# Score matmuls over 128 rows instead of alternating 64 and 128, and the decay tiles filled by ScalarE plus an adding DMA, in a hybrid decoder layer

## The chip, the cores and the metric

The kernel runs on one core of a Trainium2 chip. The metric is the device time of one execution in microseconds (us), the median of several runs. The core has TensorE (PE: matmuls, and PEld: the loads of their stationary operand), VectorE (DVE), ScalarE (ACT), GpSimd (POOL) and SyncE (SP, which here only issues DMAs). Each engine works through its own list of instructions in order, and engines wait for one another through semaphores.

## The reference

One decoder layer on 256 tokens of 1024 features, float32: a SwiGLU block, then a Mamba-2 mixer (SSD) beside sparse attention (DSA), a cross-attention to a memory, and a second SwiGLU block. The change touches two places of it:

```python
# SSD: decays between the tokens of a chunk of 128, 16 heads
a_cs = jnp.cumsum(a, axis=-1)
decay_in = jnp.exp(segsum(a))                 # exp(a_cs[l] - a_cs[s])
y_diag = jnp.einsum('bclgn,bcsgn->...', ...)  # uses decay_in
...
# DSA: index scores of 16 heads, then attention over the selected keys, 16 heads of 64
logits = jax.nn.relu(jnp.einsum('bqhd,bsd->bqhs', qi, k_idx))
score = jnp.einsum('bqhs,bqh->bqs', logits, wi)
_, idx = lax.top_k(score, topk)
s = jnp.einsum('bqhr,bqkr->bqhk', ql, sel)    # scores of the attention heads
p = jax.nn.softmax(s, axis=-1)
```

## The kernel before

Every float32 operand is split on the chip into hi (rounded to float32r) and lo = a - hi, and a product is the sum hi.hi + hi.lo + lo.hi, so an ordinary product is a chain of three matmuls per block of 128 rows. Weights arrive in pieces of 128x1024 (`raw`, 4 buffers), are cast by ScalarE to `whi` and completed by VectorE (sometimes GpSimd) to `wlo` (6 buffers of each, line 146); one piece feeds 24 matmuls. A scheduler orders the instructions of each engine at build time; several streams of work (`fly`) are emitted interleaved so that TensorE has projections to do while VectorE and ScalarE work.

The scores (`scores`, line 646) are computed for 16 index heads and later 16 attention heads. A head has 64 features. Its query tile holds hi on one half of the 128 partitions and lo on the other, and the hi part of the key stands on both halves; so for each of two token blocks one matmul over 128 rows makes hi.hi + lo.hi, and a second matmul over 64 rows adds hi.lo. The order on TensorE is 128, 64, 128, 64 rows for each head, all into one PSUM tile `ps_s` (2 buffers). An index head then needs a ReLU on ScalarE and two accumulations on VectorE into `acc` (line 669); after the 16th head VectorE selects the top 64 (lines 675 to 678). An attention head needs an addition, two maxima and a scaling on VectorE (lines 692 to 700), and two exponentials on ScalarE.

`keys_values` (line 748) makes the keys and values of four attention heads, four times: `kh` on both partition halves, `kl` on the half where the query's hi part stands, and the values `vh`, `vl` in the rest of the same buffer `kv`.

`ssd_decay` (line 508) makes the two decay tiles `E` of 128x2048: the cumulated decays `cs` are turned, written to DRAM as rows (`cs_rows`), read back onto every partition by a DMA, and GpSimd subtracts the partition's own value. VectorE then takes min(E, 0) (line 573), ScalarE the exponential (line 578), VectorE multiplies (line 580), and TensorE uses E as a stationary operand.

Of the kernel before, what the change touches and what calls it, by code (L numbers as in the profile page):

```python
"""Hybrid decoder layer (macaron SwiGLU, Mamba-2 SSD beside DSA attention, memory
cross-attention, SwiGLU; DeepNorm post-LayerNorms) on one core.

float32 products go through the tensor engine as three float32r passes: every
operand a is split on the chip into hi (a rounded to float32r) and lo = a - hi,
and a.b = hi.hi + hi.lo + lo.hi accumulates in PSUM.  Small products stay float32.
"""
# [12 lines left out]
F32 = mybir.dt.float32  # L20
F32R = mybir.dt.float32r
AF = mybir.ActivationFunctionType
ALU = mybir.AluOpType
AX = mybir.AxisListType

P = 128
T = 256
# [5 lines left out]
H = 16  # L33
HD = 64
# [4 lines left out]
ALPHA = 2.0 ** 0.25  # L39
# [11 lines left out]
class Layer:  # L51
# [37 lines left out]
    def weight(self, ap, piece=1024, pool=False):  # L89
        """loads, split into (hi, lo) in pieces of columns; pool: GpSimd makes the last lo."""  # L90
# [26 lines left out]
    def fly(self, *streams):  # L117
        """emits several streams of work in one order: a stream yields after a piece either
        how long (us of matmul work) its next piece should wait for the other engines, or the
        name of a result that another stream marks as done."""  # L120
# [17 lines left out]
    def mm3(self, out, a, b, start, stop):  # L138
        """out (+)= a^T b; a, b = (hi, lo)."""
        self.mm(out, a[0], b[0], start, False)  # L140
        self.mm(out, a[0], b[1], False, False)
        self.mm(out, a[1], b[0], False, stop)
# [5 lines left out]
    def a_block(self, ps, w, xT):  # L148
        """w: (hi, lo) [p, 128] per K block, stationary; ps [128 features, 256 tokens]."""
        for k, wk in enumerate(w):  # L150
            self.mm3(ps, wk, (xT[0][:, k, :], xT[1][:, k, :]), k == 0, k == len(w) - 1)

    def a_unit(self, ap, xT):
        """two 128-column blocks, [p, (2, kb, 128)], by 256 tokens in one bank."""
# [11 lines left out]
    def b_part(self, ps, w, xT, tb, k, start, stop):  # L166
        """tokens of block tb stationary, one K block w (hi, lo) [p, n] moving."""
# [11 lines left out]
    def b_chunk(self, wap, xT, evac, width=512):  # L179
        """[2, p, (4 kb, width)] columns, both token blocks in turn."""  # L180
# [32 lines left out]
    def constants(self):  # L213
# [7 lines left out]
        # attention keys: [0:256] for the queries of block 1, [256:384] for block 0  # L221
# [27 lines left out]
    def ln_params(self, i):  # L249
        """(scale, shift) of layer norm i, each as two halves of the columns."""  # L250
# [14 lines left out]
    def layer_norm(self, r, st, gb, dst):  # L265
        """r [128, 1024] with bn statistics st; dst may be r."""
# [11 lines left out]
    def res_evac(self, ps, c, r, x, scale, st):  # L278
        """r = scale * ps + x in the columns from c, with their statistics."""
# [11 lines left out]
    def ffn_in(self, win, xT, slots, first=None, by_token=0):  # L291
        """silu(gate) * up as hi/lo by features; the first by_token units run one token block
        after the other, so that the matmuls need not wait for the second."""
# [35 lines left out]
    def first_units(self, xT):  # L329
        """tokens and the first two units of FFN 1 K block by K block, as they arrive; the  # L330
        tensor engine and the activation tables are warmed up meanwhile."""
# [32 lines left out]
    def ffn_out(self, wout, act, finish, skew=3, last=False):  # L364
        """last: the columns that end last are finished in two parts."""
# [27 lines left out]
    def z_proj(self, xT):  # L393
        """silu(z), token-major; block 0 of the tokens runs ahead."""
# [12 lines left out]
    def xbc(self, xT, xtok, bc):  # L407
        """convolution and silu by features; x goes back to token-major."""
# [30 lines left out]
    def small_proj(self, xT):  # L439
        """c_kv, dt, w_idx and k_idx, token-major."""  # L440
# [17 lines left out]
    def latent(self, cT):  # L458
        """normalised c^T as hi/lo."""
# [18 lines left out]
    def k_index(self, kidx):  # L478
        """k_idx^T on both halves of the partitions."""
# [7 lines left out]
    def softplus(self, x, n):  # L487
        """log(1 + exp(x)) = max(x, 0) + 2 atanh(e / (2 + e)), e = exp(-|x|), x [128, n]."""
# [19 lines left out]
    def ssd_decay(self):  # L508
        """dt, the cumulated decays, and these as rows on every partition (DMA)."""
# [21 lines left out]
        scr = self.dp.tile([NTB, H * P], F32, name="cs_rows")  # L531
        self.E = []
        for tb in range(NTB):
            nc.gpsimd.dma_start(scr[tb].rearrange("(h l) -> h l", l=P), csT[:, tb, :])
            e = self.big((7, 9)[tb], F32, (P, H, P), "E")
            nc.gpsimd.dma_start(e.rearrange("p h l -> p (h l)"), scr[tb].partition_broadcast(P))
            nc.gpsimd.tensor_tensor(e, e, cs[:, tb, :].unsqueeze(2).to_broadcast([P, H, P]), op=ALU.subtract)
            self.E.append(e)

    def ssd(self, zs, xtok, bc, yT):  # L540
        """y takes the place of x in xtok."""
# [85 lines left out]
    def dsa(self, xT, kidx, cT, oT):  # L627
        """index scores, top-k, attention over the selected keys; o^T as hi/lo."""
# [4 lines left out]
        def project(name, u, scale):  # L633
            """(hi; lo) of the even heads and (lo; hi) of the odd ones on the partition halves."""
# [11 lines left out]
        def scores(q, hh, kh, kl):  # L646
            """kh: hi on both partition halves, kl: lo."""
            r, q = slice((hh % 2) * HD, (hh % 2 + 1) * HD), q[hh % 2]
            ps = self.psum("s")
            for tb in range(NTB):  # L650
                o, ts = ps[:, (1 - tb) * 256:(2 - tb) * 256], slice(tb * P, (tb + 1) * P)
                self.mm(o, q[:, hh // 2, ts], kh, True, False)
                self.mm(o, q[r, hh // 2, ts], kl[r], False, True)
# [25 lines left out]
        # attention  # L679
# [7 lines left out]
        def softmax_in(h):  # L687
            u, hh = h // 4, h % 4
            kv = self.kv[u]
            ps = scores(qs[u], hh, kv[0][:, hh % 2, hh // 2, :], kv[1][:, hh // 2, :])  # L690
# [11 lines left out]
        def turn(h):  # L702
            """p^T: key block 0 by all queries as hi/lo, key block 1 by the queries of block 1."""
# [10 lines left out]
        def values(h):  # L714
# [6 lines left out]
            # both heads of a pair are stationary, one of them is meant  # L721
# [328 lines left out]
```

## Time and profile before

| | us |
|---|---|
| three runs, median (lowest to highest) | 835.6 (834.26 to 835.91) |
| profiled execution: its own time, which is its span from the first to the last instruction | 833.3 |
| median less span | 2.3 |
| TensorE busy | 816.3 (98%) |
| VectorE busy | 560.8 (67%) |
| ScalarE busy | 424.1 (51%) |
| GpSimd busy | 68.1 (8%) |

The shares are means over stages with different limits. TensorE is busy nearly always, but a matmul's duration in the trace covers its whole passage through the array, and matmuls overlap; what a matmul costs is the distance from its start to the start of the next one.

### The profile page before, as it was taken

What the parts mean: (1) busy time and instruction counts of PE and PEld (TensorE: products, weight loads), DVE (VectorE), ACT (ScalarE), POOL (GpSimd) and SP (SyncE); (2) the same over time, 40 slices, a digit from 0 to 9 for tenths busy, and PEclk for the clock granted to TensorE, in tenths of its full rate; (3) what the DMA queues carried; (4) which work ended last, traced back from release to release, by engine and by line L of the source; (5) the groups of instructions that cost most, each with busy time, mean ns of one, the idle gap of its engine ahead of it and who ended that gap; (6) DMA issues with size and microseconds to landing.
All of it is one profiled execution on the core that took longest, in us unless ns stands there. A gap on an engine that the chain in (4) does not pass through costs nothing.

```text
span 833.3 us, 14320 instructions
## 1 busy us (share of the span) xinstructions
PE 816.3 (98%) x5726; PEld 758.1 (91%) x5726; DVE 560.8 (67%) x870; ACT 424.1 (51%) x700; POOL 68.1 (8%) x69
## 2 busy tenths in 40 slices
PE   8999999999989899999999999999999999999996
PEld 7999999887889887899999998889988999999885
DVE  5665555449598988598778767965659755555445
ACT  5564444324666584477566545454444644444430
POOL 1100000000024351130000000100001000000000
PEclk9999999999999998999999999999999999999998
DMA  7886555554556513226444355685434755555531
GB/s 246 275 281 212 178 181 184 194 176 130 193 191 240 180 49 107 72 77 217 150 126 153 117 174 182 199 271 172 151 119 134 260 184 179 187 190 179 185 120 51
DMA packets 39923, 142.97 MB, mean 172 GB/s; under 512 B 4592, under 2 KB 4896, under 8 KB 39472
## 3 DMA queue, kind: packets, MB, share of 16 engines
q1 hardware_dynamic: 38016, 134.63, 49.0%
q0 software_dynamic: 1840, 7.43, 2.9%
q8 instruction: 45, 0.74, 0.4%
q14 instruction: 22, 0.18, 0.1%
HBM read 140.97 MB, written 1.06 MB: 170 GB/s over the span
## 4 chain that ended last, share of the span: by engine, by line
PE 89%; DVE 4%; issue 4%; DMA 1%; ACT 1%; POOL 0%; SPq 0%; DVEq 0%; ACTq 0%; POOLq 0%
PE ps_mm L111 79%; PE ps_s L111 5%; DVE wlo L146 2%; PE ps_t L115 2%; PE ps_t L111 2%; DMA raw<-in_ffn_in_dram 1%; DVE wa L430 1%; ACT whi L145 0%; DVE spp L503 0%; DVE bcT L430 0%; POOL rstd L262 0%; DVE bst L285 0%; ACT L432 0%; SPq L349 0%; DVE x L282 0%
## 5 line engine op out<-in xcount | busy, mean ns | idle before, releaser
L146 DVE TENSOR_TENSOR wlo<-raw,whi 128x1024 fp32r<-128x1024 f32 (+2 forms) x245 | 302.2, 1236 | 184.8 <-ACT whi L145 183.3
L145 ACT CAST whi<-raw 128x1024 fp32r<-128x1024 f32 (+2 forms) x253 | 262.4, 1041 | 222.1 <-PE ps_mm L111 111.5
L111 PE MATMUL ps_mm<-x1Th,whi 128*128 128x256 f32 x384 | 112.4, 293 | 0.0
L111 PE MATMUL ps_mm<-x1Tl,whi 128*128 128x256 f32 x384 | 110.9, 289 | 0.0
L111 PE MATMUL ps_mm<-x1Th,wlo 128*128 128x256 f32 x384 | 110.8, 289 | 0.0
L111 PE MATMUL ps_mm<-x0Th,whi 128*128 128x256 f32 x352 | 99.7, 285 | 1.4 <-ACT whi L145 1.3
L111 PE MATMUL ps_mm<-x0Tl,whi 128*128 128x256 f32 x352 | 99.2, 283 | 0.0
L111 PE MATMUL ps_mm<-x0Th,wlo 128*128 128x256 f32 x352 | 98.3, 284 | 0.7 <-DVE wlo L146 0.7
L111 PE MATMUL ps_mm<-x3Th,whi 128*128 128x256 f32 x304 | 86.2, 284 | 0.0
L111 PE MATMUL ps_mm<-x3Th,wlo 128*128 128x256 f32 x304 | 86.0, 283 | 0.0
L111 PE MATMUL ps_mm<-x3Tl,whi 128*128 128x256 f32 x304 | 86.0, 283 | 0.0
L111 PEld LDWEIGHTS ps_mm<-x1Th,whi 128*128 128x128 f32 x384 | 75.5, 197 | 1.3
L111 PEld LDWEIGHTS ps_mm<-x1Tl,whi 128*128 128x128 f32 x384 | 75.5, 197 | 0.4 <-issue 0.4
L111 PEld LDWEIGHTS ps_mm<-x1Th,wlo 128*128 128x128 f32 x384 | 75.7, 197 | 0.1
L111 PEld LDWEIGHTS ps_mm<-x0Th,whi 128*128 128x128 f32 x352 | 67.7, 192 | 2.5 <-ACT whi L145 2.5
L111 PEld LDWEIGHTS ps_mm<-x0Th,wlo 128*128 128x128 f32 x352 | 66.9, 192 | 1.3 <-DVE wlo L146 1.3
L111 PEld LDWEIGHTS ps_mm<-x0Tl,whi 128*128 128x128 f32 x352 | 67.7, 192 | 0.0
L111 PE MATMUL ps_mm<-whi,ah 128*128 128x512 f32 x154 | 60.4, 392 | 0.0
L111 PE MATMUL ps_mm<-wlo,ah 128*128 128x512 f32 x154 | 60.1, 390 | 0.0
L111 PE MATMUL ps_mm<-whi,al 128*128 128x512 f32 x154 | 59.9, 389 | 0.0
L111 PEld LDWEIGHTS ps_mm<-x3Tl,whi 128*128 128x128 f32 x304 | 58.4, 192 | 0.0
L111 PEld LDWEIGHTS ps_mm<-x3Th,wlo 128*128 128x128 f32 x304 | 58.4, 192 | 0.0
(305 smaller groups left out, 1708.9 us busy)
## 6 DMA issues: line engine op xcount, KB each, us to landing
raw<-in_ffn_in_dram SPq DMA_DIRECT2D x87, 512.0 KB, 4.4
raw<-in_ffn_out_dram SPq DMA_DIRECT2D x44, 512.0 KB, 4.4
raw<-in_w_xbc_dram SPq DMA_DIRECT2D x16, 512.0 KB, 4.3
raw<-in_w_gate_dram SPq DMA_DIRECT2D x16, 512.0 KB, 3.6
raw<-in_w_z_dram SPq DMA_DIRECT2D x8, 512.0 KB, 4.4
raw<-in_w_qidx_dram SPq DMA_DIRECT2D x8, 512.0 KB, 4.1
raw<-in_w_q_dram SPq DMA_DIRECT2D x8, 512.0 KB, 3.7
raw<-in_w_pssd_dram SPq DMA_DIRECT2D x8, 512.0 KB, 4.1
```

Of the source, the lines that this page charges most:

```text
L111: self.nc.tensor.matmul(out, a, b, start=start, stop=stop)
L115: self.nc.tensor.transpose(out, in_, self.ident)
L145: self.nc.scalar.copy(hi, src)
L146: (engine or self.nc.vector).tensor_sub(lo, src, hi.bitcast(F32))
L430: self.last_conv = nc.vector.scalar_tensor_tensor(v[:, d:], src[:, :T - d], cw[:, 3 - d:4 - d], v[:, d:], op0=ALU.mult, op1=ALU.add)
```

## The change

In `scores` the second matmul of each token block runs over all 128 rows, with `kl` now on both partition halves; it then also adds lo.lo. In `keys_values` `kl` takes twice the columns, VectorE writes it twice (once for each half), and the values move from the `kv` buffer to a tile of the tag `w2c` (2 buffers, used once before by `btok` of the SSD). In `ssd_decay` ScalarE fills `E` with -cs, and the DMA that brings the rows adds them onto it; the GpSimd subtraction is gone.

```diff
         for tb in range(NTB):
             nc.gpsimd.dma_start(scr[tb].rearrange("(h l) -> h l", l=P), csT[:, tb, :])
             e = self.big((7, 9)[tb], F32, (P, H, P), "E")
-            nc.gpsimd.dma_start(e.rearrange("p h l -> p (h l)"), scr[tb].partition_broadcast(P))
-            nc.gpsimd.tensor_tensor(e, e, cs[:, tb, :].unsqueeze(2).to_broadcast([P, H, P]), op=ALU.subtract)
+            nc.scalar.mul(e, cs[:, tb, :].unsqueeze(2).to_broadcast([P, H, P]), -1.0)
+            nc.gpsimd.dma_start(e.rearrange("p h l -> p (h l)"), scr[tb].partition_broadcast(P), accum_op=ALU.add)
             self.E.append(e)
...
         def scores(q, hh, kh, kl):
-            r, q = slice((hh % 2) * HD, (hh % 2 + 1) * HD), q[hh % 2]
+            q = q[hh % 2]
             ps = self.psum("s")
             for tb in range(NTB):
                 o, ts = ps[:, (1 - tb) * 256:(2 - tb) * 256], slice(tb * P, (tb + 1) * P)
                 self.mm(o, q[:, hh // 2, ts], kh, True, False)
-                self.mm(o, q[r, hh // 2, ts], kl[r], False, True)
+                self.mm(o, q[:, hh // 2, ts], kl, False, True)
...
-            ps = scores(qs[u], hh, kv[0][:, hh % 2, hh // 2, :], kv[1][:, hh // 2, :])
+            ps = scores(qs[u], hh, kv[0][:, hh % 2, hh // 2, :], kv[1][:, hh % 2, hh // 2, :])
...
-        kl = s[:, 1024:1536].rearrange("p (a b) -> p a b", b=T)
-        vh, vl = s[:, 1536:1792], s[:, 1792:]
+        kl = s[:, 1024:].rearrange("p (i a b) -> p i a b", i=2, b=T)
+        v0 = self.small([P, 2, T], "w2c", F32R, 2)
+        vh, vl = v0[:, 0, :], v0[:, 1, :]
...
             nc.scalar.copy(kh[a, i], ps[a])
-            nc.vector.tensor_sub(kl[a], ps[a], kh[a, i].bitcast(F32))
             nc.scalar.copy(kh[b, i], ps[a])
+            nc.vector.tensor_sub(kl[a, i], ps[a], kh[a, i].bitcast(F32))
+            nc.vector.tensor_sub(kl[b, i], ps[a], kh[a, i].bitcast(F32))
```

Apart from line numbers and names, TensorE's order stays as it was but for a few transposes that move by some rows. The other engines' lists move at three places. ScalarE, in the convolution stage (`whi` is a weight cast, `bcT` the convolution, `E` the decay tile); before:

```order
L474 ACTIVATE cTh_2316<-ps_t_2578,feat 128x128
L428 ACTIVATE bcT_2321<-ps_mm_2513,feat 128x256
L432 ACTIVATE bcT_2321<-bcT_2321 128x256
L474 ACTIVATE cTh_2316<-ps_t_2578,feat 128x128
L145 CAST whi_2828<-raw_2827 128x1024
L432 ACTIVATE bcT_2321<-bcT_2321 128x256
L428 ACTIVATE bcT_2321<-ps_mm_2513,feat 128x256
L145 CAST whi_2834<-raw_2833 128x1024
```

and of the change, from the same row on:

```order
L474 ACTIVATE cTh_2316<-ps_t_2578,feat 128x128
L428 ACTIVATE bcT_2321<-ps_mm_2513,feat 128x256
L537 ACTIVATE E_2639<-cs_2576 128x2048
L432 ACTIVATE bcT_2321<-bcT_2321 128x256
L474 ACTIVATE cTh_2316<-ps_t_2578,feat 128x128
L432 ACTIVATE bcT_2321<-bcT_2321 128x256
L428 ACTIVATE bcT_2321<-ps_mm_2513,feat 128x256
L537 ACTIVATE E_2643<-cs_2576 128x2048
L432 ACTIVATE bcT_2321<-bcT_2321 128x256
L428 ACTIVATE bcT_2321<-ps_mm_2595,feat 128x256
L145 CAST whi_2828<-raw_2827 128x1024
L145 CAST whi_2834<-raw_2833 128x1024
```

The two fills stand ahead of two weight casts, which move behind them and behind two more rows of the convolution. GpSimd at the same place, as a difference (`cs_rows` is the scratch in DRAM, `xdt` the next work of the SSD):

```order
-L534 DMA cs_rows<-wa_2633 16x128 x2
-L536 DMA E_2639<-cs_rows 128x2048
-L536 DMA E_2643<-cs_rows 128x2048
-L537 TENSOR_TENSOR E_2639<-E_2639,cs_2576 128x2048
+L535 DMA cs_rows<-wa_2633 16x128 x2
+L538 DMA E_2639<-cs_rows 128x2048
+L538 DMA E_2643<-cs_rows 128x2048
 L146 TENSOR_TENSOR wlo_2916<-raw_2914,whi_2915 128x1024
-L537 TENSOR_TENSOR E_2643<-E_2643,cs_2576 128x2048
```

The two DMAs keep their place and the two subtractions go. VectorE where the first group of keys is made (`kv` from `ps_mm` are the keys, `acc` the index accumulation); before:

```order
L765 TENSOR_TENSOR kv_3204<-ps_mm_3206,kv_3204 64x512
L669 SCALAR_TENSOR_TENSOR acc_3015<-wa_3230,widx_2227,acc_3015 128x256
L669 SCALAR_TENSOR_TENSOR acc_3015<-wa_3230,widx_2227,acc_3015 128x128
L146 TENSOR_TENSOR kv_3204<-ps_mm_3234,kv_3204 128x256
L669 SCALAR_TENSOR_TENSOR acc_3015<-wa_3255,widx_2227,acc_3015 128x256
L669 SCALAR_TENSOR_TENSOR acc_3015<-wa_3255,widx_2227,acc_3015 128x128
L765 TENSOR_TENSOR kv_3204<-ps_mm_3206,kv_3204 64x512
```

and of the change:

```order
L768 TENSOR_TENSOR kv_3204<-ps_mm_3207,kv_3204 64x512
L769 TENSOR_TENSOR kv_3204<-ps_mm_3207,kv_3204 64x512
L670 SCALAR_TENSOR_TENSOR acc_3015<-wa_3233,widx_2227,acc_3015 128x256
L670 SCALAR_TENSOR_TENSOR acc_3015<-wa_3233,widx_2227,acc_3015 128x128
L146 TENSOR_TENSOR w2c_3205<-ps_mm_3237,w2c_3205 128x256
L670 SCALAR_TENSOR_TENSOR acc_3015<-wa_3258,widx_2227,acc_3015 128x256
L670 SCALAR_TENSOR_TENSOR acc_3015<-wa_3258,widx_2227,acc_3015 128x128
L768 TENSOR_TENSOR kv_3204<-ps_mm_3207,kv_3204 64x512
L769 TENSOR_TENSOR kv_3204<-ps_mm_3207,kv_3204 64x512
```

Two subtractions of 64x512 per group of keys have become four.

## Rows read from the trace of the kernel before

**Rows 1.** The page: the chain that ended last, share of the span by line.

```profile
PE ps_mm L111 79%; PE ps_s L111 5%; DVE wlo L146 2%; PE ps_t L115 2%; PE ps_t L111 2%; DMA raw<-in_ffn_in_dram 1%; DVE wa L430 1%; ACT whi L145 0%; DVE spp L503 0%; DVE bcT L430 0%; POOL rstd L262 0%; DVE bst L285 0%; ACT L432 0%; SPq L349 0%; DVE x L282 0%
```

**Rows 2.** Timeline of TensorE, one index head: start, duration, operation, rows*columns.

```profile
302.66 0.28 PE L111 MATMUL ps_s<-kidxh,w2a 128*128 128x256 f32 x1
302.87 0.38 PE L111 MATMUL ps_s<-kidxl,w2a 64*128 64x256 f32 x1
303.18 0.38 PE L111 MATMUL ps_s<-kidxh,w2a 128*128 128x256 f32 x1
303.49 0.38 PE L111 MATMUL ps_s<-kidxl,w2a 64*128 64x256 f32 x1
303.80 0.39 PE L111 MATMUL ps_mm<-whi,cTh 128*128 128x256 f32 x1
304.03 0.28 PE L111 MATMUL ps_mm<-wlo,cTh 128*128 128x256 f32 x1
```

**Rows 3.** Timeline of TensorE, one attention head (its four matmuls merged).

```profile
366.90 1.21 PE L111 MATMUL ps_s<-kv,w2a 128*128 128x256 f32 x4
...
368.27 0.28 PE L111 MATMUL ps_mm<-x1Tl,whi 128*128 128x256 f32 x1
```

**Rows 4.** The tile ps_s: one of its four pairs of query and key.

```profile
L111 PE MATMUL ps_s<-kv,w2a x32: 279/381/385, 366.9 to 463.4; 128*128 128x256 f32 x16, 64*128 64x256 f32 x16
```

**Rows 5.** Timeline of TensorE, scores of the cross-attention, all over 128 rows.

```profile
571.64 0.28 PE L111 MATMUL ps_s<-mkh,w2a 128*128 128x256 f32 x1
571.76 0.27 PE L111 MATMUL ps_s<-mkl,w2a 128*128 128x256 f32 x1
```

**Rows 6.** Windows: length, busy (count) of PE, PEld, DVE, ACT, POOL; granted clock; DMA.

```profile
316.00:324.00 8.00, 8.00 (x32) 6.49 (x32) 5.74 (x9) 2.89 (x5) 2.24 (x1) 0.57 0.13 48
324.00:326.00 2.00, 2.00 (x19) 2.00 (x18) 2.00 (x4) 0.00 (x0) 0.36 (x1) 1.00 0.00 0
346.00:352.00 6.00, 6.00 (x30) 5.16 (x31) 2.63 (x6) 2.62 (x8) 1.42 (x1) 0.72 0.00 0
```

**Rows 7.** Timeline of GpSimd: the two subtractions.

```profile
266.03 3.61 POOL L537 TENSOR_TENSOR E<-E,cs 128x2048 f32<-128x2048 f32 x1 [5.64 <-DMA E<-cs_rows]
...
272.91 4.59 POOL L537 TENSOR_TENSOR E<-E,cs 128x2048 f32<-128x2048 f32 x1
```

**Rows 8.** Timeline of VectorE: weight pieces beside them and after.

```profile
266.53 4.20 DVE L146 TENSOR_TENSOR wlo<-raw,whi 128x1024 fp32r<-128x1024 f32 x1 [0.90 <-ACT whi L145]
...
275.37 3.21 DVE L146 TENSOR_TENSOR wlo<-raw,whi 128x1024 fp32r<-128x1024 f32 x1
...
279.93 1.22 DVE L146 TENSOR_TENSOR wlo<-raw,whi 128x1024 fp32r<-128x1024 f32 x1
```

**Rows 9.** Waits of TensorE, 240 to 300 us: total, times, longest.

```profile
PE ps_t L115 <- ACT wa L432: 2.7, 2, 1.5
```

**Rows 10.** The tile E: its DMAs from issue to landing, VectorE's first use.

```profile
L536 POOL DMA_DIRECT2D E<-cs_rows x2: 535/550/564, 259.3 to 259.9; - x2
L573 DVE TENSOR_SCALAR E<-E x2: 1218/1222/1227, 291.9 to 295.0; 128x2048 f32<-128x2048 f32 x2
...
DMA to landing us min/median/max: 6.7/8.5/10.4
```

**Rows 11.** Windows by stage: convolution, index heads, top-k, attention heads.

```profile
245.00:297.00 52.00, 48.71 (x389) 47.55 (x390) 45.10 (x66) 33.17 (x62) 17.83 (x9) 0.97 0.57 200
297.00:351.00 54.00, 54.00 (x309) 44.33 (x308) 42.18 (x61) 28.02 (x51) 15.03 (x8) 0.91 0.22 69
351.00:366.90 15.90, 15.90 (x135) 15.90 (x135) 14.00 (x60) 11.63 (x25) 3.40 (x2) 1.00 0.20 67
366.90:470.00 103.10, 103.10 (x767) 94.92 (x766) 83.64 (x178) 68.44 (x166) 5.58 (x5) 1.00 0.46 146
```

**Rows 12.** Groups by line and shape: busy, mean ns; VectorE's keys, 297 to 470 us.

```profile
L765 DVE TENSOR_TENSOR kv<-ps_mm,kv 64x512 fp32r<-64x512 f32 x8 | 5.5, 688 | 0.4 <-ACT kv L764 0.2
```

**Rows 13.** Groups by line on the page: ScalarE's weight casts.

```profile
L145 ACT CAST whi<-raw 128x1024 fp32r<-128x1024 f32 (+2 forms) x253 | 262.4, 1041 | 222.1 <-PE ps_mm L111 111.5
```

## The prediction

> **What bounds the kernel now.** I read four views. The chain of work that ended last comes first: TensorE's matmuls make it up nearly alone, `ps_mm` with 79% and the scores' `ps_s` with 5% [rows 1]. 5% of 833.3 us is 42 us, while the kernel has few score matmuls, so the second view is TensorE's timeline at a head, where the distances between starts count. In an index head the four matmuls start at 302.66, 302.87, 303.18 and 303.49, the matmul behind them at 303.80 and the next at 304.03 [rows 2]. The distances are 0.21, 0.31, 0.31, 0.31 and 0.23 us. Every one of the 0.31 lies between a matmul over 64 rows and one over 128. The cross-attention's scores have the same 256 columns and also write several matmuls into one `ps_s`, but all over 128 rows, and start 0.12 us apart [rows 5]. So the price belongs to the alternation and not to the tile written. The attention heads show the same: from 366.90 to 368.27 pass 1.37 us for five distances [rows 3].
>
> The third view is the windows by stage, since what TensorE gives up helps only where nobody else is late. Between 297 and 351 (index heads) VectorE is busy for 42.2 of 54.0 us, in the top-k stretch for 14.0 of 15.9, between 366.9 and 470 (attention heads) for 83.6 of 103.1 [rows 11]. TensorE has no idle time there. The fourth view, waits in the convolution stage, shows TensorE waiting 2.7 us for ScalarE's `wa` [rows 9].
>
> **The change part by part.** *Scores.* 16 index and 16 attention heads with four matmuls each; one of the four query-key pairs is shown with its 16 matmuls of 64 rows among 32 [rows 4]. A head now costs 1.37 us from its first start to the second start behind it [rows 2, 3]; five distances of 0.12 [rows 5] are 0.60. That saves 0.77 us a head, 32 x 0.77 = 24.6 us. The bounds are nothing (if the price stays) and 24.6; I take 24.6, because a row of the same shape at 0.12 exists. The extra 64 rows add no columns.
>
> The Trainium skill, TensorEngine Tiling (Array Packing), section Tiling Modes, says that changing the tiling mode drains TensorE; by that the whole 24.6 us goes, and the trace agrees with 0.31 against 0.12 us [rows 2, 5]. The same section speaks against the change too: tiles of half the rows can run in parallel; by that a small matmul would hide beside its neighbour and the term would be a loss of 64 x 0.12 = 7.7 us, which is weighed as a rival.
>
> *Clock.* Twice in the index stage the granted clock drops to the lower level: between 316 and 324 us its mean is 0.57, between 346 and 352 it is 0.72 [rows 6]. With 0.5 for 1.2 GHz and 1.0 for 2.4 GHz that is (1 - 0.57)/0.5 x 8 = 6.9 and (1 - 0.72)/0.5 x 6 = 3.4 us at the lower level, 10.3 together, and up to half of it, 5.1 us, comes back if the clock holds. Each drop follows heads in which TensorE mostly switches. 32 matmuls started in the 8 us of the drop, 19 in the 2 us behind it [rows 6]. The bounds are 0 and 5.1; I take 4.0, as the heads get dense but a new wait can thin them again.
>
> *Decay tile, what goes.* GpSimd's two subtractions took 3.61 and 4.59 us [rows 7]. Beside them VectorE's weight pieces took 4.20 and 3.21 us instead of 1.22 [rows 8]: 3.0 + 2.0 = 5.0 us lost on VectorE, behind which the convolution, ScalarE's `wa` and TensorE's transposes stood. TensorE's wait of 2.7 us [rows 9] is the most that can come back.
>
> The Trainium skill, SBUF — State Buffer, section Who interferes with whom, says that a VectorE instruction with two SBUF inputs and a GpSimd instruction that reads SBUF exclude each other for a whole instruction. By that VectorE could have lost up to 3.61 + 4.59 = 8.2 us instead of 5.0; TensorE's own wait would still cap the gain.
>
> *Decay tile, what comes.* ScalarE fills 2 x 128x2048. No such row exists; twice the cast of 128x1024 is 2 x 1.04 = 2.1 us [rows 13], half of that the lower bound, twice the upper. I take 2.1, so 4.2 for both. ScalarE is busy for 33.2 of 52 us in that stage [rows 11], and the two weight casts moved behind the fills have six buffers in a row ahead of TensorE, each worth 24 matmuls or 2.9 us. What it delays is the convolution; I charge 0.5 (0 to 2.7). The convolution stage gives 2.7 - 0.5 = 2.2. The DMAs must now also read their target. They were issued at 259.3 and 259.9 and took up to 10.4 us; VectorE first touches E at 291.9 [rows 10]. The fills let them start at about 260 as before, so there are some 29 us of cover (2.7 us of an earlier stage taken off). I cost them at nothing; if the cover is gone VectorE stands at line 573 with weight pieces queued behind it.
>
> The Trainium skill, Collectives: The Full Stack, section Stop ④ — SDMA + CCE: where bytes move and the add happens, describes an add in the DMA as two reads and one write; an estimate from that is 2 x 10.4 = 21 us, still inside the cover.
>
> *Keys.* VectorE's 8 subtractions of 64x512 at 0.69 us [rows 12] become 16: +5.5 us, 1.4 of it in the index stage (one group of four), 4.1 in the attention stage. The move of the values to `w2c` costs nothing: the tile's earlier user is done long before the second group of keys.
>
> *What is late next.* That is VectorE. The index stage shrinks for TensorE to 54.0 - 16 x 0.77 - 4.0 = 37.7 us, and VectorE wants 42.2 + 1.4 = 43.6: it is 5.9 us short. The attention stage shrinks to 103.1 - 12.3 = 90.8, and VectorE wants 83.6 + 4.1 = 87.7, tight but inside. Part of the shortfall can be carried, since weight pieces are made several ahead; against that VectorE idles 11.8 us in the index stage today [rows 11], and some of it waits for results that only TensorE and ScalarE give. The bounds are 0 (all carried) and 16.3 (the index stage gains nothing: 12.3 + 4.0). I take 7.0, just above the plain shortfall.
>
> **The sum.** Against the profiled execution: 833.3 - 24.6 - 4.0 - 2.2 + 7.0 = 809.5 us of span. The median of the runs shown lies 2.3 us above the span, so 811.8 us, 2.8% less.
>
> **The rivals.** *VectorE sets the index stage.* TensorE's gain there is waited away at the `ps_s`, `wa` and `ps_mm` buffers: 7.0 becomes 16.3, 821.1 us. For it speak 43.6 against 37.7 us; against it the weight pieces held ahead. *Nothing is felt of VectorE.* 7.0 becomes 0, 804.8 us; with the whole clock and the whole convolution wait (1.1 + 0.5) 803.2. Against it the same two numbers. *The adding DMA is late.* Past 29 us from issue VectorE waits at line 573, and TensorE once its pieces run out, up to 15 us later (five pieces of 2.9). To eat the 24 us as well takes about 29 + 15 + 24 = 68 us, 6.5 times 10.4: from there on the kernel is slower. At 8 times, 83 us, it gives 835.6 + 15 = 851 us. No row shows an adding DMA; two of them share the 16 engines with weights. *The switch is not the price.* Then only the convolution gain stays, 835.6 - 2.2 = 833.4 us; 0.12 us between full-row scores [rows 5] speaks against it. *Half-row matmuls overlap their neighbours*, so that widening 64 of them costs their full 0.12 each: 835.6 + 7.7 - 2.2 = 841 us. The trace shows 0.31 instead [rows 2], so this has next to no chance. The rule on parallel tiles is that of the Trainium skill, TensorEngine Tiling (Array Packing), section Tiling Modes; the trace disagrees here, where a neighbour always uses all rows.
>
> **How the numbers follow.** Chances: forecast 0.62; VectorE sets the index stage 0.18; nothing felt 0.07; adding DMA late 0.06; switch not the price 0.05; overlap 0.02. 0.2% of 835.6, about what a measurement of this kernel can tell from no change, is 1.7 us. Faster: 0.62 + 0.18 + 0.07 and about half of the case at 833.4, 0.89; same 0.04; slower 0.07. The range goes from 803 (nothing lost) to 826 (the second case's 821.1, with the convolution's 2.2 lost and 2.7 more paid for the fills), which leaves about 0.2 outside.
>
> **What the profile after would show.** The scores' `ps_s` at 0.12 us and the chain's share of `ps_s` near 2%; granted clock 1.0 between 300 and 350; weight pieces of VectorE at 1.22 us throughout the convolution stage and no wait of TensorE for `wa`; 16 key subtractions; VectorE over 90% busy through the heads, and TensorE with a few us of new idle time there, released by VectorE or by ScalarE behind it. The prediction is wrong if the spacing stays at 0.31, if E lands later than about 289 us, or if TensorE's new idle time between 290 and 470 exceeds some 12 us.

## The result, and the profile after

The changed kernel takes 826.56 us (median of 4 runs, 825.77 to 828.1), the kernel before 835.75 us (834.26 to 837.31): a ratio of 0.9898, 95% interval 0.9877 to 0.9919. The profiled execution spans 824.7 us, the one before 833.3. The sign of the prediction holds; its 811.8 us is 14.8 us too low, and 826.56 lies just above its range (803 to 826).

The scores do what they should. The page's chain by line, which answers to [rows 1]:

```profile
PE ps_mm L111 70%; DVE wlo L146 2%; PE ps_t L111 2%; PE ps_t L115 2%; DMA raw<-in_w_qidx_dram 2%; PE ps_s L111 1%; ACT whi L145 1%; DMA raw<-in_ffn_in_dram 1%; DVE acc L670 1%; DVE acc L677 1%; DVE m L676 1%; POOL rstd L262 0%; DVE kv L769 0%; DVE kv L768 0%; ACT E L537 0%
```

`ps_s` falls from 5% to 1%. New in the chain are a weight load (`raw<-in_w_qidx_dram`, 2%) and VectorE's `acc`. TensorE's timeline at an index head, which answers to [rows 2]:

```profile
301.84 0.28 PE L111 MATMUL ps_s<-kidxh,w2a 128*128 128x256 f32 x1
301.96 0.27 PE L111 MATMUL ps_s<-kidxl,w2a 128*128 128x256 f32 x1
302.07 0.28 PE L111 MATMUL ps_s<-kidxh,w2a 128*128 128x256 f32 x1
302.19 0.28 PE L111 MATMUL ps_s<-kidxl,w2a 128*128 128x256 f32 x1
```

The starts lie 0.12 us apart, where three of the distances were 0.31. The attention head of [rows 3] (four matmuls merged, 0.71 us in place of 1.21), with a wait ahead of it:

```profile
366.63 0.71 PE L111 MATMUL ps_s<-kv,w2a 128*128 128x256 f32 x4 [1.25 <-DVE w2a L643]
```

To see where the time went, I take the start of the same matmul in both traces. After less before is -0.1 us at 253 us, 6.7 at 277, 4.4 at 293, -1.7 at 366, -0.8 at 382 and -8.7 at 471, and does not move from there to the end. So the convolution stage loses 4.5 us, the index heads and top-k stretch behind them give 6.1, the entry into the attention stage takes 0.9 and the attention stage gives 7.9.

**The loss.** The chain of waits of the changed kernel between 255 and 300 us (start, us, what):

```profile
261.50 13.72 DMA raw<-in_w_qidx_dram
...
275.32 1.04 ACT whi L145
...
276.73 0.41 ACT wa L432
```

A weight load is under way for 13.7 us, behind it come ScalarE's cast, ScalarE's `wa` in the same queue, and TensorE. The tile of these loads, first in the kernel before, then in the changed one (who waited for it, and time to landing):

```profile
  ACT whi L145: 0.5, 1
...
DMA to landing us min/median/max: 3.2/4.1/8.4
```

```profile
  ACT whi L145: 9.1, 2
...
DMA to landing us min/median/max: 3.6/8.1/13.7
```

The tile E of the changed kernel, which answers to [rows 10]:

```profile
L537 ACT ACTIVATE E<-cs x2: 1907/1909/1911, 252.0 to 255.1; 128x2048 f32<-128x2048 f32 x2
L538 POOL DMA_DIRECT2D E<-cs_rows x2: 928/1080/1231, 258.4 to 259.0; - x2
L574 DVE TENSOR_SCALAR E<-E x2: 1218/1222/1227, 296.3 to 299.4; 128x2048 f32<-128x2048 f32 x2
...
DMA to landing us min/median/max: 9.8/12.6/15.3
```

E itself is in time: the later DMA lands at 259.0 + 15.3 = 274.3, VectorE first reads E at 296.3. What is late is what shares the DMA engines with it. TensorE's waits between 240 and 300 us (answers to [rows 9]) and its timeline there:

```profile
PE ps_t L115 <- ACT wa L432: 5.6, 2, 3.1
```

```profile
274.22 0.44 PE L115 MATMUL ps_t<-ident,wa 128*128 128x128 f32 x2 [3.06 <-ACT wa L432]
277.19 0.69 PE L115 MATMUL ps_t<-ident,wa 128*128 128x128 f32 x2 [2.54 <-ACT wa L432]
...
278.10 0.41 PE L111 MATMUL ps_mm<-x1Th,wlo 128*128 128x256 f32 x1
278.32 0.41 PE L111 MATMUL ps_mm<-x1Th,whi 128*128 128x256 f32 x1
```

The wait is 5.6 us in place of 2.7, and behind it matmuls start 0.21 us apart until 282.2: the granted clock is at its lower level (0.50 from 276.0 to 282.4 us). 22 matmuls at 0.21 for 0.12 are 2 us; with 2.9 us of more wait that is near the stage's 4.5.

**The missing gain.** Windows of the changed kernel (length, busy of PE, PEld, DVE, ACT, POOL, granted clock, DMA), and under them two of the kernel before:

```profile
303.00:336.00 33.00, 29.40 (x219) 28.78 (x218) 31.61 (x44) 19.76 (x34) 9.44 (x5) 0.91 0.18 60
319.50:323.00 3.50, 3.50 (x20) 3.50 (x19) 3.44 (x6) 1.24 (x3) 0.00 (x0) 0.56 0.47 154
332.00:344.00 12.00, 10.98 (x51) 10.53 (x50) 8.22 (x15) 4.42 (x8) 0.00 (x0) 0.57 0.45 159
```

```profile
300.00:316.00 16.00, 16.00 (x104) 13.34 (x102) 15.78 (x20) 11.07 (x18) 5.65 (x3) 1.00 0.04 10
303.00:336.00 33.00, 33.00 (x186) 27.05 (x187) 28.65 (x42) 17.72 (x28) 6.91 (x4) 0.90 0.29 92
```

From 303 to 336 VectorE is busy for 31.6 of 33 us, and TensorE stands still for 3.6. The lower clock is not gone: (1 - 0.56)/0.5 x 3.5 = 3.1 and (1 - 0.57)/0.5 x 12 = 10.3 us, 13.4 together where [rows 6] gave 10.3. TensorE's longest waits from 297 to 470 us, where there were none (with three smaller ones, 0.7, 0.4 and 0.3, they come to 7.1 us), and VectorE's keys (answers to [rows 12]):

```profile
PE ps_s L111 <- ACT wa L667: 2.6, 1, 2.6
PE ps_s L111 <- DVE w2a L643: 1.3, 1, 1.3
PE ps_mm L111 <- ACT S0xe L588: 1.0, 1, 1.0
PE ps_t L115 <- DVE yTl L204: 0.8, 1, 0.8
```

```profile
L768 DVE TENSOR_TENSOR kv<-ps_mm,kv 64x512 fp32r<-64x512 f32 x8 | 5.5, 689 | 0.7 <-ACT kv L767 0.4
L769 DVE TENSOR_TENSOR kv<-ps_mm,kv 64x512 fp32r<-64x512 f32 x8 | 5.5, 688 | 0.1
```

The first wait names ScalarE, but ScalarE's timeline shows it waiting for VectorE's second subtraction of the keys, with the ReLUs behind it:

```profile
315.20 0.58 ACT L766 CAST kv<-ps_mm 64x512 fp32r<-64x512 f32 x1 [3.41 <-DVE kv L769]
```

### The profile page after: what moved, and what is told of

The parts are those of the page before. It is cut to its first block, busy times and chain, and to the rows that moved or that the text cites. A ratio compares the mean times of both kernels' runs of the same rounds, so it can differ in the third digit from the quotient of the medians.

```text
span 824.7 us, 14320 instructions
## 1 busy us (share of the span) xinstructions
PE 798.3 (97%) x5726; PEld 755.8 (92%) x5726; DVE 558.9 (68%) x878; ACT 425.1 (52%) x702; POOL 60.2 (7%) x67
## 4 chain that ended last, share of the span: by engine, by line
PE 75%; DVE 9%; issue 8%; ACT 4%; DMA 3%; POOL 1%; SPq 0%; DVEq 0%; ACTq 0%; POOLq 0%
PE ps_mm L111 70%; DVE wlo L146 2%; PE ps_t L111 2%; PE ps_t L115 2%; DMA raw<-in_w_qidx_dram 2%; PE ps_s L111 1%; ACT whi L145 1%; DMA raw<-in_ffn_in_dram 1%; DVE acc L670 1%; DVE acc L677 1%; DVE m L676 1%; POOL rstd L262 0%; DVE kv L769 0%; DVE kv L768 0%; ACT E L537 0%
## 5 line engine op out<-in xcount | busy, mean ns | idle before, releaser
L146 DVE TENSOR_TENSOR wlo<-raw,whi 128x1024 fp32r<-128x1024 f32 (+2 forms) x245 | 297.2, 1216 | 185.1 <-ACT whi L145 182.2
```

Of the source, the lines that this page charges most:

```text
L146: (engine or self.nc.vector).tensor_sub(lo, src, hi.bitcast(F32))
```

## The experiments

Two questions: what delays the weight loads (theory A: the decay part, A1 its adding DMAs, A2 its fills that push casts back), and what withholds the gain of the heads (theory V: VectorE's amount of work; rivals: the order on ScalarE, the clock). The table gives median, ratio to the kernel before with its interval, and what each stage gained (-) or lost (+) in the profiled execution, by the starts of the same matmuls as above: convolution (253 to 293 us of the kernel before), index heads and top-k (to 366), entry (to 382), attention (to 471). Each row of columns comes from one execution. Kernels with the same decay code differ by up to 2 us in the first column, e12 by more. In e13 TensorE's order differs at 382 us: a score head stands 3.4 us ahead of the `wa` transposes that go before it in the kernel before; its entry ends at those transposes (381.76 us before, 376.85 in e13).

| run | us | ratio | convolution | index, top-k | entry | attention |
|---|---|---|---|---|---|---|
| changed kernel | 826.56 | 0.9898 (0.9877 to 0.9919) | +4.5 | -6.1 | +0.9 | -7.9 |
| e1 scores only | 823.08 | 0.9831 (0.9786 to 0.9876) | +0.5 | -6.1 | +0.9 | -7.7 |
| e2 decay only | 837.29 | 1.0012 (0.9992 to 1.0032) | +3.7 | -1.4 | 0.0 | 0.0 |
| e3 plain DMA | 819.19 | 0.9802 (0.9759 to 0.9845) | -2.3 | -6.2 | +1.0 | -7.5 |
| e4 fill on GpSimd | 827.83 | 0.9897 (0.9856 to 0.9938) | +6.2 | -6.1 | +0.9 | -7.8 |
| e5 copies first | 823.63 | 0.9857 (0.9837 to 0.9877) | 0.0 | -3.9 | +0.9 | -7.2 |
| e6 GpSimd copies | 826.81 | 0.9895 (0.9879 to 0.9912) | -0.3 | -2.9 | +3.7 | -10.1 |
| e7 narrow mask | 817.30 | 0.9782 (0.9760 to 0.9804) | +0.5 | -11.7 | +3.4 | -9.1 |
| e8 one adding DMA | 822.28 | 0.9824 (0.9795 to 0.9854) | +0.2 | -7.8 | +0.9 | -7.7 |
| e9 index only | 834.22 | 0.9981 (0.9968 to 0.9993) | +0.1 | -8.7 | +6.0 | 0.0 |
| e10 attention only | 827.04 | 0.9894 (0.9869 to 0.9919) | +0.1 | 0.0 | -1.3 | -7.7 |
| e11 late filler | 825.77 | 0.9876 (0.9860 to 0.9893) | -1.0 | -5.8 | +3.9 | -9.1 |
| e12 both fillers | 830.73 | 0.9925 (0.9897 to 0.9953) | +3.0 | 0.0 | +2.8 | -8.8 |
| e13 weights on ScalarE | 820.95 | 0.9814 (0.9767 to 0.9862) | +1.1 | -9.9 | +3.7 | -8.4 |
| e14 half of them | 817.39 | 0.9782 (0.9733 to 0.9831) | -0.6 | -10.2 | +1.0 | -9.0 |

**e1 and e2, the two parts alone.** Each is the kernel before with one part of the diff.

> The score part of the change alone: 128 rows in every score matmul and the doubled keys, the decay tiles as in the kernel before (plain DMA, two GpSimd subtractions). Theory A, the decay part loses some 7 us in the convolution stage and the scores give the rest: the stage ends where it did before, the 8.4 us of the index stage and the 7.0 us of the attention stage stay, so 835.8 - 15.4 = 820 us (817 to 822). Theory B, part of the index stage's gain was only VectorE catching up during the stall ahead of it: the loss goes, but as much of the gain goes too, 825 to 828 us, like the changed kernel. Theory C, the recorded one: VectorE's shortfall alone made the miss, the decay part gains 2.2 us: 828 to 830 us.

> The decay part of the change alone: ScalarE's fills and the adding DMAs, the score matmuls and keys as in the kernel before. Theory A: slower by the stall of the convolution stage, about 6 to 7 us, 840 to 843 us, four weight loads issued at 260 to 266 us landing 12 to 14 us later. Theory B (the stall gives something back even without the scores): 836 to 839 us. Theory C: 833 to 834 us, the convolution stage gains 2.2 us.

The loss of the convolution stage comes and goes with the decay part (theory A), and the recorded theory C, a gain of 2.2 us from it, falls. With the scores the decay part costs 826.56 - 823.08 = 3.5 us. By itself it makes no difference that can be told, as the medians go (1.4 us, the interval holds 1): there the stage loses 3.7 us in the trace and the stretch behind gives 1.4 back. That is theory B's range for e2, but B falls for e1: the index column is the same 6.1 us with the stall and without it. E1's median lies 1 us above A's range.

**e3 and e4, adding or fill.**

```diff
-            nc.gpsimd.dma_start(e..., scr[tb].partition_broadcast(P), accum_op=ALU.add)
+            nc.gpsimd.dma_start(e..., scr[tb].partition_broadcast(P))                    # e3
...
-            nc.scalar.mul(e, cs[...].to_broadcast([P, H, P]), -1.0)
+            nc.gpsimd.tensor_scalar(e, cs[...].to_broadcast([P, H, P]), -1.0, None, op0=ALU.mult)   # e4
```

> The changed kernel with plain DMAs into the decay tiles in place of the adding ones, order of all engines the same; this leaves out the subtraction of the token's own decay. Theory A1, the adding DMAs hold the 16 DMA engines about twice as long and the weight loads behind them land late: the two decay DMAs land within 11 us of issue as before, the four weight loads within 9 us, TensorE's stall shrinks from 7 to 0 to 2 us, 819 to 822 us. Theory A2, the fills are the cause, since they push two weight casts back and so free the weight buffers 4 us later (first load issued at 260.0 in place of 256.0): the stall stays at 5 to 7 us, 824 to 827 us.

> The changed kernel with the two fills on GpSimd in place of ScalarE; ScalarE's weight casts go back to their place before the change and the adding DMAs stay, some microseconds later. Theory A1 (the adding DMAs alone are enough): the loads issued beside them still land 10 to 14 us after issue and TensorE still stalls 4 to 7 us, 823 to 827 us. Theory A2 (the order of ScalarE is the cause): the loads issued from 256 us on are there in time and the stall is 0 to 2 us although the DMAs add, 819 to 822 us.

In e3 all engines keep the order of the changed kernel, fills included, and only the addition is gone. Its decay tiles, its weight loads and TensorE's wait in the convolution stage:

```profile
DMA to landing us min/median/max: 4.8/6.7/8.6
```

```profile
DMA to landing us min/median/max: 3.1/5.1/8.3
```

```profile
PE ps_t L115 <- ACT wa L432: 1.2, 1, 1.2
```

The queue that carries the decay tiles, from 258 to 276 us: packets, MB and the time its packets took as a share of 16 engines, in the changed kernel and in the kernel before:

```profile
q0 software_dynamic: 288, 2.10, 57.2%
```

```profile
q0 software_dynamic: 288, 2.10, 28.5%
```

The same 2.10 MB held the DMA engines for 10.3 us of the 18 in place of 5.1. The four weight loads issued beside them landed 11.8 to 13.7 us after issue in the changed kernel, 6.0 to 8.3 in e3. So A1 is shown: 7.4 us lie between the two kernels, 6.8 of the profiled ones in the convolution column, and A2 (a stall of 5 to 7 us without the addition) falls: with the fills and no addition the wait is 1.2 us. The fills may still share in the loss: the first of the four loads is issued at 260.0 us in the changed kernel, behind the adding DMAs, and at 256.0 in the kernel before, ahead of the decay DMAs. What the addition costs with the casts in their old place is not shown. E4 comes out near A1 (0.8 us above its range) but tells less than it should: GpSimd's fills took 5.4 us each, held up its weight piece behind them and with it the loads, so that these were issued later than in any other kernel.

**e5 and e6, the order of the keys, and GpSimd for VectorE's second subtraction.**

```diff
             nc.scalar.copy(kh[a, i], ps[a])
             nc.scalar.copy(kh[b, i], ps[a])
+        for i in range(2):
+            a, b = ...
             nc.vector.tensor_sub(kl[a, i], ps[a], kh[a, i].bitcast(F32))
-            nc.vector.tensor_sub(kl[b, i], ps[a], kh[a, i].bitcast(F32))
+            nc.gpsimd.tensor_copy(kl[b, i], kl[a, i])        # e6 alone
```

> The score part alone (decay tiles as before), with ScalarE's four key copies of a group written ahead of VectorE's four subtractions. In the score part alone ScalarE stood 3.4 us at the third copy until VectorE's second subtraction was done, with the ReLUs behind it, and TensorE then 2.6 us for a ReLU. Theory S, that order makes the wait: ScalarE no longer waits for VectorE there, TensorE's 2.6 us go and some of the lower clock behind them, 3 to 4 us less than the score part alone, 818 to 820 us. Theory V, VectorE is behind as a whole between about 300 and 335 us and any order waits for it: 822 to 824 us, the wait reappears at another instruction.

> As the run with the copies first, and the second half of kl is copied by GpSimd from the first half in place of VectorE's second subtraction: VectorE has 8 instructions of 0.69 us less, 1.4 us in the index stage and 4.1 us in the attention stage. Theory V: the index stage gains 1.4 us or more and the attention stage 1 to 3 us beyond the run with the copies first, 817 to 821 us. Rival G, GpSimd's copies come late or hold VectorE up: no gain, 822 to 826 us.

E5 keeps VectorE's work and takes ScalarE's wait away. TensorE's longest wait in it from 297 to 470 us:

```profile
PE ps_mm L111 <- ACT S0xe L588: 3.8, 1, 3.8
```

The 2.6 us at the ReLU are gone, and 3.8 stand some 10 us further on, at `S0xe`: theory S falls, as the time is that of e1. E6 took 8 subtractions off VectorE and got slower: TensorE waits 5.2 us for a ReLU and 3.1 for `yTl`. The GpSimd copies come behind VectorE's subtraction, each 0.6 us and a turn later. The ReLU is late because ScalarE stands still ahead of it:

```profile
329.74 0.59 ACT L642 ACTIVATE w2e<-ps_mm 64x512 fp32r<-64x512 f32 x1 [6.67 <-DVE w2a L643]
```

VectorE made that `w2a` only at 329.0 us, behind five accumulations (3.7 us) and three weight pieces (3.5 us). So less work on VectorE did not help while its order put this work first.

**e7, less VectorE work.**

```diff
-                nc.vector.tensor_tensor(ev, ev, cbm[...].to_broadcast([P, 2, H // G, P]), op=ALU.mult)
+                nc.vector.tensor_tensor(ev[..., :8], ev[..., :8], cbm[..., :8].to_broadcast([P, 2, H // G, 8]), op=ALU.mult)
```

> The score part alone, with VectorE's multiplication of the decay tiles by the masked products cut to the first 8 of every 128 columns (the rest of the product is left out): VectorE has some 5.5 us less to do in the index stage. Theory V: TensorE's waits of 2.6, 1.3 and 1.0 us in the index stage shrink or go, the clock drops less, the stage takes 4 to 7 us less than in the score part alone, 816 to 819 us. Rival N, the stage's missing gain is the clock or ScalarE's own load: under 1.5 us, 821.5 to 824 us.

The index column goes from -6.1 to -11.7, 5.6 us. VectorE's multiplication (line 581) took 1.7 us in place of 5.9, 4.2 less and not 5.5. How that becomes 5.6 shows at ScalarE's `w2e`, first in e1, then in e7, and in the windows behind it:

```profile
328.95 0.59 ACT L642 ACTIVATE w2e<-ps_mm 64x512 fp32r<-64x512 f32 x1 [2.77 <-DVE w2a L643]
```

```profile
327.08 0.59 ACT L642 ACTIVATE w2e<-ps_mm 64x512 fp32r<-64x512 f32 x1 [0.16 <-DVE w2a L643]
```

```profile
333.00:344.00 11.00, 11.00 (x49) 10.28 (x49) 7.05 (x12) 3.00 (x8) 0.00 (x0) 0.54 0.16 55
```

```profile
333.00:344.00 11.00, 10.97 (x88) 10.53 (x87) 8.65 (x16) 6.74 (x21) 1.42 (x1) 1.00 0.01 2
```

In e1 ScalarE stands 2.8 us for VectorE, TensorE then 1.0 us for `S0xe`, and behind that wait (1 - 0.54)/0.5 x 11 = 10.1 us pass at the lower clock, which cost half of it, 5.1 us. In e7 the wait and the drop are gone. So VectorE's lateness is at the root, as theory V has it, but most of the gain is clock, as rival N named it, and that it comes near the work taken off is chance. The intervals of e7 and e1 overlap by a little (0.9804 and 0.9786); the medians are 5.8 us apart. The next wait is VectorE's again, 2.1 us for `yTl` at the entry.

**e8, one decay tile of each kind.**

```diff
+            if tb == 1:
+                nc.scalar.mul(e, ..., -1.0)
+                nc.gpsimd.dma_start(e..., accum_op=ALU.add)
+            else:
                 nc.gpsimd.dma_start(e..., ...)
                 nc.gpsimd.tensor_tensor(e, e, cs[...], op=ALU.subtract)
```

> The score part with one decay tile of each kind: the first by a plain DMA and GpSimd's subtraction, the second by a fill and an adding DMA. Theory A1 (the time on the DMA engines is the price, in proportion to the bytes added): the weight loads beside them land some 3 us earlier than with two adding DMAs, the convolution stage loses 1 to 4 us, 821 to 825 us, between the score part alone and the whole change. Rival: the price is a threshold (the weight pieces held ahead cover one adding DMA wholly) and one GpSimd subtraction less frees VectorE: 818 to 821 us, faster than the score part alone.

With one adding DMA and one GpSimd subtraction the stage loses +0.2, with two adding DMAs 4.5, and of the four kernels built on e8 three lie at -1.0 to +1.1 and e12 at +3.0. E8 also has one GpSimd subtraction less than e1; if half of the 2.8 us between e1 (+0.5) and e3 (-2.3) is its gain, the one addition costs about 1 us (an estimate) where two cost 6.8. So it is not in proportion but as the rival had it. The loads are late in e8 too, but not all, and TensorE waits 2.7 us for `wa` as before. ScalarE's waits for them (total, times, longest) and their landing:

```profile
ACT whi L145 <- DMA raw<-in_w_qidx_dram: 7.8, 3, 2.8
```

```profile
DMA to landing us min/median/max: 3.2/5.3/12.4
```

The longest wait is 2.8 us where the changed kernel has 8.4. Two reasons are possible, and neither was tried by itself: the pieces held ahead cover just one adding DMA, or it matters that with one fill the first load is issued ahead of the decay DMAs again (258.4 us). The time lies in A1's range all the same, as no gain over e1 can be told, 822.28 to 823.08 us with overlapping intervals. Both beat the changed kernel.

**e9 and e10, the two kinds of heads alone**, on the kernel before, with its decay tiles:

```diff
-                self.mm(o, q[r, hh // 2, ts], kl[r], False, True)
+                rows = slice(0, P) if full else r          # full: index heads in e9, attention heads in e10
+                self.mm(o, q[rows, hh // 2, ts], kl[rows], False, True)
```

> The kernel before with 128 rows in the second matmuls of the 16 index heads alone (their low keys already stood on both halves); attention heads, keys and decay tiles as before. In every run with the score part the index stage gave 6.1 us. Theory V (VectorE's work sets that stage): without the second subtraction of the keys VectorE has 1.4 us less there, so the stage gives about 7.5 us, and nothing moves elsewhere: 827 to 829.5 us. Rival: the keys' second subtraction is not what binds, the stage gives 6 us again, 830 us or a little less. If the whole of the dense heads' gain came through, 12.3 us, it would be 824.

> The kernel before with 128 rows in the attention heads' second matmuls and the doubled keys; the index heads keep 64 rows, the decay tiles stay as before. Theory V: the attention stage gives the same 6.6 to 7.0 us as in the runs with both, since its limit is its own VectorE work; the index stage, where TensorE is still slow, hides the 1.4 us of keys: 828.5 to 830 us. Rival: the attention stage starts later or earlier against VectorE's backlog from the index stage and so gives more by itself, 8 to 10 us, 826 to 828.

The 6.1 us that this text takes as the mark held for the changed kernel, e1, e3 and e4; e5, e6 and e8 gave 3.9, 2.9 and 7.8. E9's index column gave 8.7 us, as V expects of less VectorE work, but 6.0 of it were lost at the entry: a wait of 2.4 us for VectorE's `yTl` at 366.4 us and the lower clock behind it.

```profile
364.00:368.00 4.00, 1.62 (x7) 1.18 (x7) 3.72 (x10) 1.88 (x7) 0.00 (x1) 0.86 0.36 131
368.00:372.00 4.00, 4.00 (x17) 3.55 (x18) 2.59 (x6) 2.17 (x7) 0.00 (x0) 0.50 0.05 14
```

So the dense index heads by themselves are worth 1.6 us of 12.3, which no theory of mine had. E10 went as its rival said: about 9 us from 366 us on. Without an earlier end of the index stage its trace has no wait for `yTl` at the entry.

**e11 and e12, the clock.** E8 with matmuls of zeros behind one or two index heads:

```diff
                 self.mm(o, q[:, hh // 2, ts], kl, False, n == 0)
+                for i in range(n):
+                    self.mm(o, self.zero.to_broadcast([P, P]), self.dist[:, :T], False, i == n - 1)
```

> The kernel with one adding DMA, and behind the four score matmuls of the 12th index head three float32 matmuls of zeros that add nothing to the sum and take about 0.43 us each, where TensorE stood idle for 1.1 us and the granted clock then fell to the lower level for some 7 to 10 us. Theory K, it is the idle time ahead that lets the clock fall: the drop behind 330 us goes or shrinks, 3 to 5 us less than the 822.3 us without them, 817 to 820 us. Rival: the clock falls all the same (what is left is the time of the fillers and a ReLU that starts later): 822 to 825 us.

> As the run before, with five such matmuls of zeros each behind the 6th and the 12th index head, to cover the wait of 2.6 us at the 7th head as well. Theory K: both drops of the clock in the index stage go, 816 to 819 us. Rival: the fillers delay the ReLUs that TensorE waits for, so that the waits grow as they are filled: 823 to 827 us.

From 330 to 345 us, e11 and then e8:

```profile
330.00:345.00 15.00, 11.78 (x81) 11.04 (x81) 13.07 (x20) 5.53 (x14) 2.75 (x1) 0.89 0.48 165
```

```profile
330.00:345.00 15.00, 15.00 (x97) 14.54 (x97) 11.62 (x23) 5.64 (x16) 1.51 (x2) 0.77 0.28 97
```

The lower clock does shrink, from 6.9 to 3.3 us, and TensorE then stands still for 3.2 us, waiting for VectorE's `xtok`: what the clock gave, the wait took. The kernel is slower than e8, as both rivals said, and both medians lie above even the rivals' ranges. E12's waits grew too (4.6 us for ReLUs), and its executions spread from 825.3 to 833.8 us.

**e13 and e14, work moved off VectorE with nothing left out**, on e8: the weighting of an index head on ScalarE, for all heads or every second one.

```diff
                 for tb, s in self.BLOCKS:
-                    nc.vector.scalar_tensor_tensor(acc[:, s], rl[:, s], self.widx[:, tb, h:h + 1], prev[:, s], ...)
+                    nc.scalar.activation(rl[:, s], rl[:, s], AF.Copy, scale=self.widx[:, tb, h:h + 1])
+                nc.vector.tensor_add(acc, rl, prev)
```

> The kernel with one adding DMA, and in each of the 16 index heads the weighting by the token's own factor moves from VectorE's two instructions (0.52 and 0.49 us) to two of ScalarE (about 0.4 us each, by the silu of 128x256), so that VectorE keeps one addition of 128x384 (0.55 us). The whole computation is kept. VectorE has some 7 us less to do between 300 and 345 us, ScalarE some 12 more. Theory V: the index stage gives 4 to 6 us more, of which the stretch behind it (where VectorE makes the top-k) takes back 1 to 3, 816 to 820 us against 822.3 us without the move. Rival: ScalarE is late in its place, or the lower clock is what withholds the gain: 822 us or more.

> As the run before, for every second index head only: VectorE has 3.6 us less, ScalarE 6 more. Theory V: half of that gain, 818.5 to 821 us. If ScalarE is what the whole move runs into, this one is the faster of the two.

The index column goes from -7.8 to -9.9 and -10.2, and the lower clock between 333 and 344 us is gone in e14:

```profile
333.00:344.00 11.00, 10.82 (x88) 10.72 (x89) 9.34 (x17) 7.64 (x24) 1.04 (x1) 1.00 0.14 48
```

E14, with half the move, has the lowest median of the kernels that compute everything, 817.39 us, 9.2 us under the changed kernel, with intervals that do not touch. Against e8 and e13 its interval overlaps (0.9733 to 0.9831; e8 0.9795 to 0.9854, e13 0.9767 to 0.9862), so that half a move beats none or a whole one is likely but not shown. E13 stays above its range: what it gained more than e8 up to the top-k is lost at the entry, where TensorE waits 2.8 us for `yTl` and the column is +3.7 against +0.9. VectorE's accumulations (18.2 us in e8) took 14.1 in e13 and 16.9 in e14, so less came off than the 7 and 3.6 us expected.

## Why the prediction was off

**Scores, 24.6 us: right.** The distance is 0.12 us in both kinds of heads, `ps_s` is out of the chain. The Trainium skill (TensorEngine Tiling (Array Packing), section Tiling Modes) says that changing the tiling mode drains TensorE; the 0.31 us that became 0.12 agree with it.

**The adding DMAs, "I cost them at nothing": wrong, and the first of the two steps that failed.** I looked only at who reads E. That cover was real: E landed 22 us before its reader. But the DMA engines are shared, and the weight loads behind had no 29 us, only the pieces held ahead. In the kernel before, a window over these microseconds shows the engines full as it was, so that no room was left for a doubled transfer could have been read:

```profile
260.00:264.00 4.00, 4.00 (x36) 4.00 (x35) 3.13 (x6) 2.99 (x6) 0.39 (x1) 1.00 0.97 324
264.00:268.00 4.00, 4.00 (x35) 4.00 (x35) 2.92 (x4) 2.21 (x5) 1.97 (x1) 1.00 1.00 412
```

The DMA share is 0.97 and 1.00. The rule named in the prediction (the Trainium skill, Collectives: The Full Stack, section Stop ④ — SDMA + CCE: where bytes move and the add happens) describes two reads and a write, and the estimate worked out from it, twice the time, agrees with the trace (57.2% for 28.5%); I applied it to the wrong customer. The rival "the adding DMA is late" had the same blind spot.

**The convolution's 2.2 us: right in mechanism, outweighed.** Without GpSimd's subtractions VectorE's pieces take 1.22 us, and e3, which has the fills and no adding, gains 2.3 us there (TensorE's wait goes from 2.7 to 1.2). That it meets the 2.2 so closely is partly luck, as kernels with the same decay code differ by up to 2 us. Adding turned it into +4.5. Together 6.7 us of the miss.

**The clock, 4.0: wrong in sign, and the second step that failed.** 10.3 us at the lower level became 13.4, half of which is 1.6 us lost; with the 4.0 forecast that is 5.6 us of the miss (2 us more are in the convolution stage). I expected dense heads to hold the clock; TensorE waited instead, and each drop of the changed kernel's heads follows a wait (begun at 315.8 and 332.1 us). The term was no independent one: where VectorE was relieved the long drop went (e7, e14), where it was not, covering the wait gained nothing (e11). What makes the clock fall stays open, for in the kernel before and in e10 it falls in the same stage with no wait of TensorE there (granted 0.57 from 316 to 324 us in the one, 0.50 from 320 to 324 in the other).

**What is late next, 7.0: right in kind, a little small.** By the forecast the three last columns should have given 12.3 + 4.0 + 12.3 - 7.0 = 21.6 us; they give 13.1, 8.5 less. 5.6 of these are the clock's; the other 2.9 make 9.9 us out of the 7.0. TensorE's new waits are 7.1 of them, at VectorE or at ScalarE behind it, as forecast; what the other 2.8 are stays open. The shortfall was worked out from a mean over 54 us (42.2 busy). But VectorE was already busy for 15.8 of the 16 us from 300 to 316 in the kernel before, and for 14.0 of 15.9 in the top-k stretch [rows 11], so next to nothing could be carried over there, and its lateness cost clock besides. E7 shows it: relieving VectorE took away a wait and with it the long drop. The rival "VectorE sets the index stage" had 16.3 us lost, and 15.5 (8.5 and the 7.0) are; that is luck in the number, since by the rival the index stage gains nothing, and it gave 6.1.

6.7 us from the convolution stage, 5.6 from the clock and 2.9 from what is late next make 15.2, the distance from 809.5 to the span of 824.7. None of the prediction's three signs of being wrong came: the spacing is 0.12 us, E landed at 274.3, the new waits are 7.1 us. None of them looked at the weight loads or at the clock; of what the profile was to show, no wait for `wa` and a granted clock of 1.0 from 300 to 350 us failed.

## What to carry to other kernels

When a DMA gets heavier, price it for the other users of the DMA engines in that stretch before asking whether its own reader can wait. When TensorE gets faster, look for the engine that is late next in slices of a few microseconds, since a mean over a stage hides the slices in which it is full already; then relieve that engine and look again, as the wait moves to the next place (e7, e13). A gain that ends at a stretch in which another engine is full can be lost there: the index heads alone (e9) were worth 8.7 us in their stage and 1.6 at the end. In e1 a wait of 1.0 us was followed by a drop of the clock that cost 5.1, so waits are to be looked at together with the granted clock behind them.

## What the runs showed that I had not expected

Two adding DMAs of 1 MB each held the DMA engines twice as long as plain ones of the same bytes (57.2% against 28.5% and, in e3, 29.8% of 18 us); with one of two adding it was 50.4%, and yet the convolution stage lost next to nothing. GpSimd's fill of 128x2048 from a broadcast operand took 5.4 us where ScalarE's took 1.91. Behind waits of TensorE of 1 to 5 us the granted clock often went to its lower level, for some 3 to 10 us and in e5 for 17 (0.57 from 323 to 343 us), while matmuls ran; in the kernel before it fell in the index stage with no wait at all. Executions of one and the same kernel differ in it (e8: 816.0 us at a mean of 0.994, 823.6 at 0.987).
